# One tile of 64 columns for the two sliver tiles of a stick-breaking attention

## The chip, the cores and the metric

The kernel runs on one core of a Trainium2 chip. The metric is the device time of one execution in microseconds (us), the median of several runs. Engines are named as the profile names them: PE is TensorE's matmul, PEld its weight load, DVE is VectorE, ACT ScalarE, POOL GpSimd, and SP issues DMAs.

## The reference, cut to what matters

The program is one inference step of a hybrid decoder layer: stick-breaking attention in 8 heads beside gated linear attention (GLA) in 4 heads, with one input projection and one output projection. The change touches the prompt's stick-breaking attention alone. There are 16 meta tokens and 1024 prompt tokens; a query sees the keys strictly before it.

```
def stick_break_weights(z, mask):
    sp = jnp.where(mask, jax.nn.softplus(z), 0.0)
    later = lax.cumsum(sp, axis=z.ndim - 1, reverse=True) - sp
    return jnp.where(mask, jnp.exp(jax.nn.log_sigmoid(z) - later), 0.0)

def sb_attend(qb, qpos, k, v, kpos, bias):
    a = stick_break_weights(sb_logits(qb, k, bias), kpos[None, :] < qpos[:, None])
    return jnp.einsum('bhqk,bkhd->bqhd', a.astype(v.dtype), v)
```

The sum `later` runs over all keys after the current one that the query sees, so key tiles are worked from the last to the first, and each tile needs one number per query from the tile before: the sum so far.

## The kernel before, in words

Sizes: 1040 positions, head width 128, eight heads `h`. The queries of a head are split in two halves `qi`: positions 16 to 527 (qi = 0) and 528 to 1039 (qi = 1), 512 columns each. The keys are cut in tiles of `KT` = 126; tile `j` lies in columns 128 j to 128 j + 127 of `kt`, with zeros in its first and last row. The first row of a tile carries the sum of the tiles before it: its mask bias is -1e30, and the lower triangular matrix `ntri0` with a full first row adds it to every key.

For a key tile that reaches past the start of a query half, only the columns of the queries that can see it are worked. Half qi = 1 has the tiles j = 8 to 0 with 32, 158, 284, 410 and then five times 512 columns; half qi = 0 has j = 4 to 0 with 24, 150, 276, 402 and 512. The tiles (1, 8), 32 columns, and (0, 4), 24 columns, are the slivers. `ORDER` (L641) lists the tiles of a head: all of qi = 1, then all of qi = 0.

One tile is one generator, `attend_tile` (L578 to L629):

- three matmuls for the logits into a PSUM tile `z` (L589 to L591; every fp32 operand is held as a high and a low part, so a product takes three matmuls),
- softplus: DVE adds the bias and caps (L595), ACT does Exp and Ln (L596, L597), DVE adds and takes the maximum (L598), POOL masks with an affine select (L601),
- the carry of the tile before, read from row 0 of its `z` by ACT (L607), and the split in two parts by ACT and DVE (`split_tmp`, L574 and L575),
- two matmuls with `ntri0` onto `z` (L610, L611): the prefix sum,
- ACT's Exp to `Y` (L615), POOL's mask (L617), and the split again,
- three matmuls with the values onto the half's output `O` (L623 to L625); after j = 0 ACT copies `O` (L628) and SP stores it to `od`.

The `z` tiles come from a tag of four PSUM banks, `O` from one bank, and three more banks hold the projections' accumulators. The transposes of K and V to tokens (`tok_out`, L541, copied by L543 to L546) and the sample products (`sample_q`, L651 and L656) use the `z` tag too. A tile's bank becomes free when its last reader is done.

Order: a `Weaver` counts beats. The main program issues the projections (`inproj`, L342 to L344; six matmuls, then one beat) and each generator says after how many beats it goes on. Attention of head h is so woven between the V, K and Q projections of head h + 1. Within a tile the steps stand 2, then `D1` = 4, then `D2` = 6 beats apart, and a tile whose predecessor's carry is not yet there steps one beat at a time. Instructions of an engine run in the order in which they were issued to it. Beside this, DVE works through the sample scores (`z_feed`, L464), tied to the projections' progress by explicit dependencies.

`load_v` (L554 to L569) fetches a head's values from the output tensor through staging buffers (`stage`, seven of them) into `V`. `head` zeroes `kt` (L681, L682), and `split_k` (L685 to L697) fills it.

Of the kernel before, what the change touches and what calls it, by code (L numbers as in the profile page):

```python
# [10 lines left out]
F32 = mybir.dt.float32  # L11
# [5 lines left out]
ALU = mybir.AluOpType  # L17
# [3 lines left out]
P = 128  # L21
# [6 lines left out]
NSMP = NB * NT  # L28
T = META + SEQ + NSMP
REAL = META + SEQ  # L30
# [10 lines left out]
KT = 126  # L41
# [43 lines left out]
def hybrid_step(ctx: ExitStack, tc: tile.TileContext, x_prompt, x_sample, cache_k, cache_v, state_gla,  # L85
# [3 lines left out]
    nc = tc.nc  # L89
    mm = nc.tensor.matmul  # L90
    vec, act, pool = nc.vector, nc.scalar, nc.gpsimd
# [17 lines left out]
    W = Weaver()  # L109

    def stage(nm, dt=F32):
        return stg.tile([P, 384], dt, tag="stg", name=nm)
# [39 lines left out]
    znd = dram.tile([NSMP, HEADS, NSMP], F32, name="znd")  # L152
# [37 lines left out]
    with tc.tile_pool(name="xp", bufs=2) as xp, tc.tile_pool(name="xps", bufs=5, space=PSUM) as xps:  # L190
# [109 lines left out]
        for c, (lo, hi) in enumerate(XCHUNKS):  # L300
            n = hi - lo
            for k in range(NK):
                ps = xps.tile([P, 512], F32, tag="tx", name=f"tx{c}_{k}")
                ks = slice(k % 8 * P, (k % 8 + 1) * P)
                for j, i in enumerate(TILES[c]):
                    xt = xts[i]
                    if len(xt) == 2:
                        src, ii = xt[k // 8][:, ks], ident[:]
                    else:
                        rs = slice(64 * (k // 8), 64 * (k // 8) + 48)  # L310
                        src, ii = xt[0][rs, ks], ident[rs, rs]
# [215 lines left out]
    with tc.tile_pool(name="sp", bufs=1) as sp, tc.tile_pool(name="sps", bufs=1, space=PSUM) as sps:  # L527
# [26 lines left out]
        def load_v(h, V, behind):  # L554

            for c in range(3):
                st = stage(f"vr{h}_{c}")
                sv = st[:].rearrange("p (a d) -> p a d", d=P)
                nt = 3 if c < 2 else 2
                src = new_v_prompt[0, 0, :, h, :]  # L560
                pool.memset(st[:], 0.0)
                nc.sync.dma_start(sv[1:KT + 1, :nt], src[c * 378:c * 378 + nt * KT].rearrange("(a p) d -> p a d", p=KT))
                if c == 2:
                    nc.sync.dma_start(sv[1:33, 2, :], src[8 * KT:REAL])
                vs = slice(3 * c, 3 * c + 3)
                ins = act.copy(V[0][:, vs, :], sv)
                tc.add_manual_dep(ins.ins, behind.name, NOSYNC, reason="behind")
                vec.tensor_tensor(V[1][:, vs, :], sv, V[0][:, vs, :].bitcast(F32), ALU.subtract)
                yield 1  # L569

        def split_tmp(X, rows, n, nm):
            a = sp.tile([P, 512], F32R, tag="hi", bufs=3, name=f"hi_{nm}")
            b = sp.tile([P, 512], F32R, tag="lo", bufs=3, name=f"lo_{nm}")
            act.copy(a[:rows, :n], X)  # L574
            vec.tensor_tensor(b[:rows, :n], X, a[:rows, :n].bitcast(F32), ALU.subtract)  # L575
            return a, b

        def attend_tile(h, qi, qlo, qhi, j, jmax, q, kt, V, carry, O):  # L578
            nm = f"{h}_{qi}_{j}"
            k0 = j * KT  # L580
            nk = P
            c0 = max(qlo, k0)
            col = c0 - qlo
            n = qhi - c0
            qs = slice(c0 - META, c0 - META + n)
            ks = slice(j * P, j * P + nk)
            z = sps.tile([P, 512], F32, tag="z", bufs=4, name=f"z{nm}")
            zz = z[:nk, :n]
            mm(zz, kt[0][:, ks], q[0][:, qs], start=True, stop=False)  # L589
            mm(zz, kt[0][:, ks], q[1][:, qs], start=False, stop=False)  # L590
            mm(zz, kt[1][:, ks], q[0][:, qs], start=False, stop=True)  # L591
            bias = bias0[:nk, h:h + 1]
            xt = sp.tile([P, 512], F32, tag="X", bufs=3, name=f"X{nm}")
            X = xt[:nk, :n]
            vec.tensor_scalar(X, zz, bias, 30.0, ALU.add, ALU.min)  # L595
            act.activation(X, X, AF.Exp)  # L596
            act.activation(X, X, AF.Ln, bias=1.0)  # L597
            vec.scalar_tensor_tensor(X, zz, bias, X, ALU.add, ALU.max)  # L598
            w = min(n, k0 + KT - c0)
            if w > 0:  # L600
                pool.affine_select(X[:, :w], X[:, :w], [[1, w]], ALU.is_gt, 0.0, base=c0 - k0 + 1, channel_multiplier=-1)  # L601
            yield 2
            if j < jmax:
                while carry.get(qi, (None,))[0] != j + 1:
                    yield 1
                _, cz, ccol = carry[qi]
                act.activation(X[0:1, ccol - col:], cz[0:1, :], AF.Copy, scale=-1.0)  # L607
            sh, sl = split_tmp(X, nk, n, "s" + nm)
            yield D1
            mm(zz, ntri0[:nk, :nk], sh[:nk, :n], start=False, stop=False, skip_group_check=True)  # L610
            mm(zz, ntri0[:nk, :nk], sl[:nk, :n], start=False, stop=True, skip_group_check=True)  # L611
            carry[qi] = (j, zz, col)
            yt = sp.tile([P, 512], F32, tag="X", bufs=3, name=f"Y{nm}")
            Y = yt[:nk, :n]
            act.activation(Y, zz, AF.Exp, bias=bias)  # L615
            if w > 0:
                pool.affine_select(Y[:, :w], Y[:, :w], [[1, w]], ALU.is_gt, 0.0, base=c0 - k0 + 1, channel_multiplier=-1)  # L617
            ah, al = split_tmp(Y, nk, n, "a" + nm)
            yield D2
            if j == jmax:  # L620
                O[qi] = sps.tile([P, 512], F32, tag="O", name=f"O{h}_{qi}")
            o = O[qi]
            mm(o[:, col:], V[0][:nk, j, :], ah[:nk, :n], start=(j == jmax), stop=False, skip_group_check=True)  # L623
            mm(o[:, col:], V[0][:nk, j, :], al[:nk, :n], start=False, stop=False, skip_group_check=True)
            mm(o[:, col:], V[1][:nk, j, :], ah[:nk, :n], start=False, stop=(j == 0), skip_group_check=True)  # L625
            if j == 0:
                st = sp.tile([P, 512], F32, tag="X", bufs=3, name=f"ost{h}_{qi}")
                act.copy(st[:], o[:])  # L628
                nc.sync.dma_start(od[h][:, qlo - META:qhi - META], st[:])  # L629

        def attend(h, q, kt, V):

            carry, O = {}, {}
            for qi, j in ORDER:
                qlo, qhi = ((16, 528), (528, REAL))[qi]
                n = qhi - max(qlo, j * KT)
                W.spawn(attend_tile(h, qi, qlo, qhi, j, (qhi - 1) // KT, q, kt, V, carry, O))
                yield 2 if n < 100 else 3 if n < 200 else 4 if n < 450 else 5

        D1, D2 = 4, 6  # L640
        ORDER = [(1, j) for j in range(8, -1, -1)] + [(0, j) for j in range(4, -1, -1)]  # L641

        def values(h, behind):
            V = [sp.tile([P, 9, P], F32R, tag=f"V{i}", name=f"V{i}_{h}") for i in range(2)]
            W.spawn(load_v(h, V, behind))
            return V

        def sample_q(h, qsm, ks):

            ps = sps.tile([P, 512], F32, tag="z", bufs=4, name=f"qst{h}")  # L650
            nc.tensor.transpose(ps[:NSMP, 0:P], qsm[:], ident[:])  # L651
            qtok = stage(f"qtok{h}")[:NSMP, :P]
            act.copy(qtok, ps[:NSMP, 0:P])
            nc.sync.dma_start(qsd[:, h * P:(h + 1) * P], qtok)
            ps = sps.tile([P, 512], F32, tag="z", bufs=4, name=f"zn{h}")
            mm(ps[:NSMP, :NSMP], ks[:], qsm[:], start=True, stop=True)  # L656
            zns = sp.tile([NSMP, NSMP], F32, tag="zns", name=f"zns{h}")
            act.copy(zns[:], ps[:NSMP, :NSMP])
            nc.sync.dma_start(znd[:, h, :], zns[:])
            yield 4  # L660
            heads_ready.append(h)

        def head(h):
# [15 lines left out]
            kt = [sp.tile([P, KW], F32R, tag=f"k{i}", name=f"k{i}_{h}") for i in range(2)]  # L679
# [3 lines left out]
            ks = sp.tile([P, NSMP], F32, tag="ks", name=f"ks{h}")  # L683

            def split_k(raw, c, lo, hi):  # L685
                at, end = lo, min(hi, REAL)
                while at < end:
                    j, off = divmod(at, KT)
                    n = max(1, (end - at) // KT) if off == 0 else 1
                    w = min(KT - off, end - at)  # L690
                    d = [t[:, j * P:(j + n) * P].rearrange("p (a x) -> p a x", a=n)[:, :, off + 1:off + 1 + w] for t in kt]
                    r = raw[:, at - lo:at - lo + n * w].rearrange("p (a x) -> p a x", a=n)
                    act.copy(d[0], r)
                    vec.tensor_tensor(d[1], r, d[0].bitcast(F32), ALU.subtract)
                    at += n * w
                if c == 2:
                    act.copy(ks[:], raw[:, REAL - lo:hi - lo])  # L697
                return
                yield
# [21 lines left out]
            V = values(h, copied[-1])  # L721
# [15 lines left out]
    with tc.tile_pool(name="gp", bufs=1) as gp, tc.tile_pool(name="gps", bufs=1, space=PSUM) as gps:  # L737
# [323 lines left out]
        for g in range(GH):  # L1061
            kt = gp.tile([P, T], F32, tag="k", name=f"gk{g}")
# [629 lines left out]
```

## Time and profile before

| | us |
|---|---|
| median of 3 runs (2065.34 to 2067.61) | 2066.58 |
| the profiled execution, its own time | 2066.38 |
| its span, first to last instruction | 2064.6 |
| first to last logits product of the attention (L589) | 116.3 to 833.0 |
| mean granted clock of TensorE | 0.999 |

The busy times are summed from instruction records. Matmul records overlap, each next one starting before the one ahead has ended, so the distance from start to start is what a matmul costs TensorE, not its duration. In rows of the timeline the first number is the start in us from the span's start, the second the duration in us; a bracket at the end names how long the engine had been idle and for what.

### The profile page before, as it was taken

How to read it: one execution, taken by the hardware profiler on the slowest of the kernel's cores; microseconds unless marked ns; L12 is line 12 of the kernel's file. 1: busy time of each engine (PE TensorE's matmuls, PEld its weight loads, DVE VectorE, ACT ScalarE, POOL GpSimd, SP SyncE). 2: the span in 40 equal slices, each digit the busy share in tenths (PEclk: the TensorE clock that was granted, in tenths of full speed). 3: DMA queues.
4: the chain of work that ended last, by engine and by line, in shares of the span. 5: the costliest groups of instructions: out<-in, count | busy, mean ns of one | idle time of the engine just before them, and what ended most of it. 6: DMA issues, size and time to landing. Idle time of an engine off the chain costs nothing.

```text
span 2064.6 us, 41985 instructions
## 1 busy us (share of the span) xinstructions
PE 2024.8 (98%) x12507; PEld 1863.6 (90%) x12507; DVE 1552.7 (75%) x6282; ACT 953.4 (46%) x2293; POOL 84.6 (4%) x304
## 2 busy tenths in 40 slices
PE   6999999999999999999999999999999999999998
PEld 5999999999999998999999999998888898788776
DVE  7368989888988989899798897978544347454576
ACT  7355555565655656433534335343433325332332
POOL 0012000101000000000000000000000000000000
PEclk9999999999999999999999999999999999999999
DMA  6354454544455442533433433335776666452485
GB/s 202 103 139 148 139 159 133 171 132 147 146 160 146 140 124 76 139 102 82 108 100 79 125 82 110 98 82 155 236 233 231 220 222 200 139 166 74 129 271 202
DMA packets 371821, 301.85 MB, mean 146 GB/s; under 512 B 42360, under 2 KB 312104, under 8 KB 371592
## 3 DMA queue, kind: packets, MB, share of 16 engines
q1 hardware_dynamic: 371288, 298.64, 48.6%
q8 instruction: 98, 1.61, 0.3%
q14 instruction: 131, 1.07, 0.2%
q10 hardware_dynamic: 304, 0.53, 0.1%
HBM read 241.75 MB, written 57.31 MB: 145 GB/s over the span
## 4 chain that ended last, share of the span: by engine, by line
PE 75%; DVE 12%; DMA 6%; ACT 3%; issue 3%; SPq 0%; POOL 0%; DVEq 0%; ACTq 0%; POOLq 0%
PE acc_g L342 5%; PE acc_g L343 5%; PE acc_g L344 5%; DVE jk L464 5%; PE b L1593 4%; PE b L1595 4%; PE b L1594 4%; PE acc_k L342 3%; PE acc_k L344 3%; PE acc_k L343 3%; PE acc_v L342 2%; PE acc_q L342 2%; PE acc_q L344 2%; PE acc_q L343 2%; PE acc_v L344 2%
## 5 line engine op out<-in xcount | busy, mean ns | idle before, releaser
L464 DVE SCALAR_TENSOR_TENSOR jk<-kp,qb 128x128 f32<-128x128 f32 x2048 | 593.8, 290 | 43.5 <-DMA qb<-qsd 1.7
L342 PE MATMUL acc_g<-hT,wh_g 128*128 128x368 f32 (+2 forms) x768 | 251.4, 327 | 0.5 <-DVE ga L389 0.5
L343 PE MATMUL acc_g<-hT,wh_g 128*128 128x368 f32 (+2 forms) x768 | 247.6, 322 | 0.0
L344 PE MATMUL acc_g<-hT,wl_g 128*128 128x368 f32 (+2 forms) x768 | 247.1, 322 | 0.0
L1593 PE MATMUL b<-ring,f 128*128 128x512 f32 x416 | 164.3, 395 | 3.5 <-ACT gx L521 1.4
L464 DVE DVE_READ_ACCUMULATOR jk<-kp,qb 128x1 f32 x2048 | 167.6, 82 | 0.0
L1594 PE MATMUL b<-ring,f 128*128 128x512 f32 x416 | 162.6, 391 | 0.0
L1595 PE MATMUL b<-ring,f 128*128 128x512 f32 x416 | 162.1, 390 | 0.0
L342 PEld LDWEIGHTS acc_g<-hT,wh_g 128*128 128x128 f32 x768 | 144.5, 188 | 13.3 <-issue 10.8
L343 PEld LDWEIGHTS acc_g<-hT,wh_g 128*128 128x128 f32 x768 | 144.6, 188 | 1.1 <-issue 0.4
L1395 DVE TENSOR_TENSOR ring<-wr,ring 128x512 fp32r<-128x512 f32 x104 | 71.3, 689 | 98.4 <-ACT ring L1394 97.7
L344 PEld LDWEIGHTS acc_g<-hT,wl_g 128*128 128x128 f32 x768 | 144.5, 188 | 0.0
L342 PE MATMUL acc_gv<-hT,wh_gv 128*128 128x400 f32 (+2 forms) x384 | 130.5, 340 | 0.0
L1394 ACT CAST ring<-wr 128x512 fp32r<-128x512 f32 x104 | 64.1, 620 | 139.3 <-PE b L1595 77.0
L342 PE MATMUL acc_k<-hT,wh_k 128*128 128x384 f32 (+1 forms) x384 | 126.4, 329 | 0.0
L343 PE MATMUL acc_gv<-hT,wh_gv 128*128 128x400 f32 (+2 forms) x384 | 125.3, 326 | 0.0
L342 PE MATMUL acc_q<-hT,wh_q 128*128 128x368 f32 (+2 forms) x384 | 125.1, 326 | 0.0
L344 PE MATMUL acc_gv<-hT,wl_gv 128*128 128x400 f32 (+2 forms) x384 | 124.8, 325 | 0.0
L344 PE MATMUL acc_k<-hT,wl_k 128*128 128x384 f32 (+1 forms) x384 | 124.7, 325 | 0.0
L343 PE MATMUL acc_k<-hT,wh_k 128*128 128x384 f32 (+1 forms) x384 | 124.5, 324 | 0.0
L344 PE MATMUL acc_q<-hT,wl_q 128*128 128x368 f32 (+2 forms) x384 | 123.4, 321 | 0.0
L343 PE MATMUL acc_q<-hT,wh_q 128*128 128x368 f32 (+2 forms) x384 | 123.4, 321 | 0.0
(454 smaller groups left out, 5294.3 us busy)
## 6 DMA issues: line engine op xcount, KB each, us to landing
kp<-in_cache_k_dram SPq DMA_DIRECT2D x512, 64.0 KB
vr<-in_cache_v_dram SPq DMA_DIRECT2D x64, 512.0 KB
tf<-in_w_out_dram SPq DMA_DIRECT2D x64, 256.0 KB
td<-tf SPq DMA_DIRECT2D x64, 256.0 KB
qb<-qsd SPq DMA_DIRECT2D x64, 256.0 KB
wr_g<-in_w_in_dram SPq DMA_DIRECT2D x64, 256.0 KB
wr<-td SPq DMA_DIRECT2D x56, 256.0 KB
wr<-in_w_out_dram SPq DMA_DIRECT2D x48, 256.0 KB
```

The source lines that it names most:

```text
L342: mm(acc[c][:, :n], wh, hh[k][:, lo:hi], start=(k == 0), stop=False)
L343: mm(acc[c][:, :n], wh, hl[k][:, lo:hi], start=False, stop=False)
L344: W.mark = mm(acc[c][:, :n], wl, hh[k][:, lo:hi], start=False, stop=(k == NK - 1)).ins
L464: ins = vec.scalar_tensor_tensor(jk[:], kp[:], 1.0, qbs[h, b][:, t, :], ALU.mult, ALU.mult, accum_out=zt[:, t, NPG - 1 - i:NPG - i])
L1394: act.copy(wh, r)
L1395: vec.tensor_tensor(wl, r, wh.bitcast(F32), ALU.subtract)
L1593: mm(bk[:], ah, wh, start=first and k == 0, stop=False, skip_group_check=True)
L1594: mm(bk[:], ah, wl, start=False, stop=False, skip_group_check=True)
L1595: mm(bk[:], al, wh, start=False, stop=last and k == 7, skip_group_check=True)
```

## The change

The two slivers become one tile, j = 8, of 64 columns: the last 32 queries of each half.

- Its keys are the last keys, in rows 1 to 31 as before (the last of all, which no query sees, drops out), and after them, in rows 32 to 55, the 24 keys 504 to 527 of tile 4. The keys are copied by POOL within `kt`, the values come by one more DMA a head (24 rows).
- Its mask is one affine select over both halves and a memset of the first half's first 32 rows, once for `X` and once for `Y`.
- Its carry serves both halves: columns 0 to 31 for (0, 3), columns 32 to 63 for (1, 7).
- Its product with the values goes to columns 256 to 319 of its own `z` bank, ACT copies that to a small tile `ob`, and for each half DVE adds 32 columns of it to the copy of `O` before the store.
- `ORDER` loses (0, 4). Tile (1, 7) is now the first that writes `O` of its half, (0, 3) that of the other.
- The small tile `zns` of the sample logits becomes a staging buffer.

```
@@ load_v
                 if c == 2:
-                    nc.sync.dma_start(sv[1:33, 2, :], src[8 * KT:REAL])
+                    nc.sync.dma_start(sv[1:32, 2, :], src[8 * KT:REAL - 1])
+                    nc.sync.dma_start(sv[32:56, 2, :], src[4 * KT:4 * KT + 24])
@@ attend_tile
+            both = j == 8
             c0 = max(qlo, k0)
             col = c0 - qlo
-            n = qhi - c0
+            n = 64 if both else qhi - c0
+            def queries(t):
+                if both:
+                    return t[:].rearrange("p (a x) -> p a x", a=2)[:, :, 480:512]
+                return t[:, qs]
+
+            def causal(t):
+                if both:
+                    t = t.rearrange("p (a x) -> p a x", a=2)
+                    pool.affine_select(t, t, [[1 - 24, 2], [1, 32]], ALU.is_gt, 0.0, base=24, channel_multiplier=-1)
+                    pool.memset(t[0:32, 0, :], 0.0)
+                elif w > 0:
+                    pool.affine_select(t[:, :w], t[:, :w], [[1, w]], ALU.is_gt, 0.0, base=c0 - k0 + 1,
+                                       channel_multiplier=-1)
...
-            if j < jmax:
+            jmax = (3, 7)[qi]
+            if not both:
                 while carry.get(qi, (None,))[0] != j + 1:
                     yield 1
...
-            carry[qi] = (j, zz, col)
+            if both:
+                carry[0], carry[1] = (4, z[:, 0:32], 480), (8, z[:, 32:64], 480)
+            else:
+                carry[qi] = (j, zz, col)
...
+            if both:
+                o = z[:, 256:320]
+                mm(o, V[0][:, j, :], ah[:, :n], start=True, stop=False, skip_group_check=True)
+                mm(o, V[0][:, j, :], al[:, :n], start=False, stop=False, skip_group_check=True)
+                mm(o, V[1][:, j, :], ah[:, :n], start=False, stop=True, skip_group_check=True)
+                O[2] = sp.tile([P, 64], F32, tag="ob", name=f"ob{h}")
+                act.copy(O[2][:], o)
+                return
...
             if j == 0:
                 st = sp.tile([P, 512], F32, tag="X", bufs=3, name=f"ost{h}_{qi}")
                 act.copy(st[:], o[:])
+                vec.tensor_tensor(st[:, 480:512], st[:, 480:512], O[2][:, 32 * qi:32 * qi + 32], ALU.add)
                 nc.sync.dma_start(od[h][:, qlo - META:qhi - META], st[:])
@@ attend
-        ORDER = [(1, j) for j in range(8, -1, -1)] + [(0, j) for j in range(4, -1, -1)]
+        ORDER = [(1, j) for j in range(8, -1, -1)] + [(0, j) for j in range(3, -1, -1)]
@@ sample_q
-            zns = sp.tile([NSMP, NSMP], F32, tag="zns", name=f"zns{h}")
-            act.copy(zns[:], ps[:NSMP, :NSMP])
-            nc.sync.dma_start(znd[:, h, :], zns[:])
+            zns = stage(f"zns{h}")[:NSMP, :NSMP]
+            act.copy(zns, ps[:NSMP, :NSMP])
+            nc.sync.dma_start(znd[:, h, :], zns)
@@ split_k
                 if c == 2:
+                    for t in kt:
+                        pool.tensor_copy(t[:, 8 * P + 32:8 * P + 56], t[:, 4 * P + 1:4 * P + 25].bitcast(F32))
                     act.copy(ks[:], raw[:, REAL - lo:hi - lo])
```

More of the change, by code (lines that the diff above doesn't have):

```diff
@@ L576, in split_tmp, with attend_tile @@
             return a, b
-        def attend_tile(h, qi, qlo, qhi, j, jmax, q, kt, V, carry, O):
+        def attend_tile(h, qi, qlo, qhi, j, q, kt, V, carry, O):
             nm = f"{h}_{qi}_{j}"
@@ L581, in attend_tile @@
             nk = P
+            both = j == 8
             c0 = max(qlo, k0)
             col = c0 - qlo
-            n = qhi - c0
+            n = 64 if both else qhi - c0
             qs = slice(c0 - META, c0 - META + n)
             ks = slice(j * P, j * P + nk)
+            def queries(t):
[10 more added lines that the diff above has]
+                                       channel_multiplier=-1)
             z = sps.tile([P, 512], F32, tag="z", bufs=4, name=f"z{nm}")
             zz = z[:nk, :n]
-            mm(zz, kt[0][:, ks], q[0][:, qs], start=True, stop=False)
-            mm(zz, kt[0][:, ks], q[1][:, qs], start=False, stop=False)
-            mm(zz, kt[1][:, ks], q[0][:, qs], start=False, stop=True)
+            mm(zz, kt[0][:, ks], queries(q[0]), start=True, stop=False)
+            mm(zz, kt[0][:, ks], queries(q[1]), start=False, stop=False)
+            mm(zz, kt[1][:, ks], queries(q[0]), start=False, stop=True)
             bias = bias0[:nk, h:h + 1]
@@ L599, in attend_tile @@
             w = min(n, k0 + KT - c0)
-            if w > 0:
-                pool.affine_select(X[:, :w], X[:, :w], [[1, w]], ALU.is_gt, 0.0, base=c0 - k0 + 1, channel_multiplier=-1)
+            causal(X)
             yield 2
-            if j < jmax:
+            jmax = (3, 7)[qi]
+            if not both:
                 while carry.get(qi, (None,))[0] != j + 1:
@@ L615, in attend_tile @@
             act.activation(Y, zz, AF.Exp, bias=bias)
-            if w > 0:
-                pool.affine_select(Y[:, :w], Y[:, :w], [[1, w]], ALU.is_gt, 0.0, base=c0 - k0 + 1, channel_multiplier=-1)
+            causal(Y)
             ah, al = split_tmp(Y, nk, n, "a" + nm)
@@ L636, in attend @@
                 n = qhi - max(qlo, j * KT)
-                W.spawn(attend_tile(h, qi, qlo, qhi, j, (qhi - 1) // KT, q, kt, V, carry, O))
+                W.spawn(attend_tile(h, qi, qlo, qhi, j, q, kt, V, carry, O))
                 yield 2 if n < 100 else 3 if n < 200 else 4 if n < 450 else 5
         D1, D2 = 4, 6
-        ORDER = [(1, j) for j in range(8, -1, -1)] + [(0, j) for j in range(4, -1, -1)]
+        ORDER = [(1, j) for j in range(8, -1, -1)] + [(0, j) for j in range(3, -1, -1)]
         def values(h, behind):
```

## The prediction

> **What bounds the kernel now.** I read the page's busy shares and chain first, then the busy time by stretch, then what TensorE waited for in the stretch that holds the attention, then single rows of that stretch in order of time.
>
> ```profile
> span 2064.6 us, 41985 instructions
> ...
> PE 2024.8 (98%) x12507; PEld 1863.6 (90%) x12507; DVE 1552.7 (75%) x6282; ACT 953.4 (46%) x2293; POOL 84.6 (4%) x304
> ...
> PE 75%; DVE 12%; DMA 6%; ACT 3%; issue 3%; SPq 0%; POOL 0%; DVEq 0%; ACTq 0%; POOLq 0%
> ```
>
> TensorE is busy in 98% of the span and has 75% of the chain that ended last. A share over the whole span proves little about one stage, so the next view cuts it: the columns are busy time and count of PE, its weight loads, DVE, ACT and POOL, then the granted clock, the DMA share and GB/s.
>
> ```profile
> 112.00:860.00 748.00, 743.03 (x4548) 711.83 (x4547) 664.79 (x3022) 430.35 (x1037) 72.06 (x249) 1.00 0.48 139
> 860.00:1400.00 540.00, 537.60 (x3653) 517.91 (x3652) 469.01 (x2316) 219.06 (x601) 0.84 (x9) 1.00 0.38 99
> 1400.00:1800.00 400.00, 395.56 (x2509) 347.28 (x2511) 207.69 (x534) 157.69 (x333) 3.60 (x15) 1.00 0.64 205
> ```
>
> The prompt attention of the eight heads runs from 116 to 852 us, woven between the projections' matmuls. There PE lacks 748.0 - 743.0 = 5.0 us of being always busy, at clock 1.00. What it waited for in that stretch:
>
> ```profile
> PE z L611 <- DVE lo_s L575: 2.5, 9, 0.8
> PE z L610 <- ACT hi_s L574: 1.7, 4, 0.9
> PE acc_g L342 <- DVE ga L389: 0.5, 1, 0.5
> ```
>
> So time taken off TensorE's queue here moves everything behind it forward, and the two stretches that follow (99.6% and 98.9% busy) hand it on to the end: the projections there are paced by the same queue. DVE, at 664.8 of 748, is the next bound, 83 us away.
>
> **What goes: one sliver tile a head.** Each of the eight heads loses tile (0, 4) with its 24 columns: three logits products, two of the prefix sum, three with the values. The rows are start, duration, engine and line; since durations overlap, the price is read from starts. Head 1's tile:
>
> ```profile
> 260.81 0.17 PE L589 MATMUL z<-q,k 128*128 128x24 f32 x1
> 260.83 0.26 PE L590 MATMUL z<-q,k 128*128 128x24 f32 x1
> 260.95 0.26 PE L591 MATMUL z<-q,k 128*128 128x24 f32 x1
> 261.06 0.42 PE L342 MATMUL acc_k<-hT,wh_k 128*128 128x384 f32 x1
> 261.32 0.34 PE L343 MATMUL acc_k<-hT,wh_k 128*128 128x384 f32 x1
> 261.49 0.33 PE L344 MATMUL acc_k<-hT,wl_k 128*128 128x384 f32 x1
> ...
> 268.82 0.17 PE L610 MATMUL z<-hi_s,ntri 128*128 128x24 f32 x1
> ...
> 268.96 0.43 PE L342 MATMUL acc_k<-hT,wh_k 128*128 128x384 f32 x1
> 269.22 0.33 PE L343 MATMUL acc_k<-hT,wh_k 128*128 128x384 f32 x1
> ...
> 276.49 0.26 PE L623 MATMUL O<-hi_a,V 128*128 128x24 f32 x1
> ...
> 276.82 0.42 PE L342 MATMUL acc_q<-hT,wh_q 128*128 128x384 f32 x1
> 277.08 0.34 PE L343 MATMUL acc_q<-hT,wh_q 128*128 128x384 f32 x1
> ```
>
> A projection product of 384 columns takes 0.17 us from start to start (261.32 to 261.49). From the first logits product to the projection's second product pass 261.32 - 260.81 = 0.51 us, of which 0.17 are the projection's own: the three cost 0.34 us. The pair of the prefix sum costs 269.22 - 268.82 - 0.17 = 0.23 us. The three with the values cost 276.82 - 276.49 = 0.33 us (the late product after them would also be late behind the transposes that stand just ahead of them). Together 0.90 us a head, 8 x 0.90 = 7.2 us. If that late product is charged too (277.08 - 276.82 - 0.17 = 0.09 us) it is 0.99, or 7.9 us in all.
>
> **What stays, now 64 columns wide.** The merged tile stands where the 32-column one stood. Nearest wider row, 158 columns with the values:
>
> ```profile
> 229.96 0.23 PE L623 MATMUL O<-hi_a,V 128*128 128x158 f32 x1
> ...
> 230.26 0.38 PE L342 MATMUL acc_v<-hT,wh_v 128*128 128x384 f32 x1
> 230.47 0.34 PE L343 MATMUL acc_v<-hT,wh_v 128*128 128x384 f32 x1
> ```
>
> 230.47 - 229.96 - 0.17 = 0.34 us: 158 columns cost what 24 do, so 64 cost nothing more. The bounds are 0 and 0.01 us for this group, under 0.3 us in all if every group grew so. I take 0.
>
> **The z bank that is held longer.** The carry of the merged tile for the first half of the queries is read only when tile (0, 3) reaches its carry, nine tiles later. Until then its z bank is not free, and z has four. So a bank that the second half's tiles, the transposes of V and the sample products shared is gone for some 50 us of each head. I laid the allocation times of head 1 and the times of the last reads beside each other with one bank less. At most points 0.7 us or more remain; at these it does not:
>
> ```profile
> 131.73 0.40 PE L589 MATMUL z<-q,k 128*128 128x512 f32 x1
> ...
> 131.97 0.29 ACT L607 ACTIVATE X<-z 1x158 f32<-1x158 f32 x1
> ...
> 503.36 0.40 PE L589 MATMUL z<-q,k 128*128 128x512 f32 x1
> ...
> 504.20 0.29 ACT L607 ACTIVATE X<-z 1x158 f32<-1x158 f32 x1
> ...
> 244.86 0.57 ACT L607 ACTIVATE X<-z 1x512 f32<-1x512 f32 x1
> ...
> 245.11 0.49 PE L541 MATMUL tk_v<-ident,vraw 128*128 128x128 f32 x3
> ...
> 246.28 0.49 PE L541 MATMUL tk_v<-ident,vraw 128*128 128x128 f32 x3
> ...
> 246.88 0.46 ACT L543 COPY st_v<-tk_v 128x384 f32<-128x384 f32 x1
> ...
> 247.32 0.39 PE L589 MATMUL z<-q,k 128*128 128x512 f32 x1
> ```
>
> Tile (1, 4) would take the bank of tile (1, 7), whose last read is the carry of 158 columns: in head 0 that ends at 132.26 and the tile starts at 131.73, 0.53 us too early; in head 4 it ends at 504.49 against 503.36, 1.13 us. And tile (1, 1), at 247.32, would need the bank that the copy of the second transposes leaves at 246.88 + 0.46 = 247.34: about even, and I charge 0.08 us for each of seven heads, an estimate. Sum 0.53 + 1.13 + 0.56 = 2.2 us of TensorE waiting. It is 0 if the order of instructions moves so that projections fill the gap. If the second transposes (245.11) get the bank whose carry read ends at 244.86 + 0.57 = 245.43, 0.32 us too late, seven heads pay 2.2 us more: 4.4 us. I take 2.2, since the repeating pattern of the heads gives the program order little reason to move.
>
> **The rest, costed at nothing, with its cover.**
>
> ```profile
> L575 DVE TENSOR_TENSOR lo_s<-X,hi_s x112: 173/578/695, 118.5 to 843.0; 128x512 fp32r<-128x512 f32 x48, 128x32 fp32r<-128x32 f32 x8, 128x158 fp32r<-128x158 f32 x8, 128x284 fp32r<-128x284 f32 x8
> ...
> L598 DVE SCALAR_TENSOR_TENSOR X<-z,bias,X x112: 238/639/752, 117.6 to 837.6; 128x512 f32<-128x512 f32 x48, 128x32 f32<-128x32 f32 x8, 128x158 f32<-128x158 f32 x8, 128x284 f32<-128x284 f32 x8
> ...
> 213.97 0.21 POOL L601 TENSOR_SCALAR_AFFINE_SELECT X<-X 128x32 f32<-128x32 f32 x1 [11.72 <-DVE X L598]
> ...
> 218.09 0.18 PE L610 MATMUL z<-hi_s,ntri 128*128 128x32 f32 x1
> ...
> 279.01 0.20 POOL L682 MEMSET k<- 128x128 f32 x1
> ...
> 298.27 0.38 SPq L629 DMA_DIRECT2D od<-ost  x1
> ```
>
> DVE loses four small operations a head (the minima above: about 0.24 + 0.24 + 0.17 + 0.17 = 0.82 us, 6.6 us in all) and gets two additions of 32 columns a head, between 0.17 and 0.24 us each, 2.7 to 3.8 us: still 3 us less. They stand between ACT's copy of O and the store to od; behind a waiting one, DVE's next operations queue, and its 83 us of idle time cover them. Without that cover it would be 16 x 0.24 = 3.8 us.
> ACT loses five operations a head and gets one copy; it idles 318 us here.
> POOL loses two selects and gets two memsets and two copies of key columns a head, each around the 0.20 us above. The memsets lengthen the merged tile's chain by some 0.2 us in front of ACT's split, twice; in head 1 the mask ended at 213.97 + 0.21 = 214.18 and the prefix sum began at 218.09, so it is hidden. The key copies queue ahead of masks of tiles (0, 1) and (0, 0); uncovered, 16 x 0.20 = 3.2 us.
> SP gets one more issue a head, at 0.38 us like the row, 3 us on a queue that mostly waits for others. The values it brings are needed only at the merged tile's last products, after both its masks and its prefix sum.
> The sample logits now leave through one of the seven staging buffers; if none were free, DVE would start a head's sample scores later. I see no such wait and take 0.
> The carry chain of the first half is one link shorter. What is late next is tile (0, 1): the waits on lo_s quoted above come mostly at its 402-column products. They may go or come back elsewhere: -3 to +3 us, taken as 0.
>
> **The sum.** -7.2 + 0 + 2.2 = -5.0 us. The profiled execution took 2066.38 us by its own time (2064.6 of span and 1.8 around it), 0.2 under the runs' median of 2066.58. From it, 2066.4 - 5.0 = 2061.4.
>
> **The rivals.**
> 1. The held bank costs nothing, because other work fills the gaps: -7.2 us, 2059.2. For it speaks that PE found work to do in nearly every gap so far; against it, that the three places above lie within about a microsecond.
> 2. The held bank starves TensorE. If the three transposes, needing a bank in close order, reuse the one just left, the third (246.28) waits for the copy that ends at 247.34, 1.06 us, and tile (1, 1) for the copy after, another 0.45 us: 1.5 us for each of seven heads, 10.6 us, on top of the 1.7 us of heads 0 and 4. -7.2 + 12.3 = +5.1, 2071.5. It decides from 0.9 us a head on, where the gain is used up. Against it: in the rows above the third transposes start before the second's copy has begun, so these two already sit on different banks.
> 3. The change saves less than it seems. The first two sliver products start 0.02 us apart; if each product cost only that, the eight heads would save 64 x 0.02 = 1.3 us, 2065.1. Against it: the second and third start 0.12 us apart, with 24 columns. [...]
> 4. The lo_s waits shrink as the chain shortens: -7.2 - 3 + 0, 2056.2.
>
> **How the numbers follow.** The forecast (2061.4, own range 2058 to 2064) gets 0.48, rival 1 gets 0.18, rival 2 0.12, rival 3 (or any other give-back that leaves about nothing) 0.14, rival 4 0.08. Two runs of this kernel can be told apart from about 0.2%, 4.1 us: faster means under 2062.4, slower over 2070.7. Of the forecast some two thirds lie under 2062.4, 0.33; with rivals 1 and 4 faster has 0.59. Slower is rival 2, 0.12. The rest, 0.29, is the same. The range runs from rival 4, 2056, to 2069, short of rival 2's centre.
>
> **What would show it.** Right: PE has 64 fewer products and weight loads, (0, 3) follows directly on (1, 0), and the stretch of the attention is 5 to 7 us shorter with the later stretches as long as before. The held bank: new waits of PE at L589 or L541 for ACT's carry copies and st_v, 2 us in sum; over 7 us of them would be rival 2. POOL's key copies ahead of a mask that lo_s waits for, or DVE waiting at the new addition with PE behind it, would show a cover that failed. A later stretch that grows by what the attention saves would mean that TensorE's queue was not what paced it.

## The result, and the profile after

| | before | changed |
|---|---|---|
| median of 12 runs each, us | 2066.53 | 2072.59 |
| ratio, 95% interval | | 1.0030 (1.0022 to 1.0038) |
| span of the profiled execution, us | 2064.6 | 2069.3 |

The changed kernel is slower by 0.3%, 6 us, where 5 us less was forecast: beyond the range, whose upper end was 2069. One of its twelve runs took 5120 us, for a reason that no trace shows, and doesn't enter the ratio. Each ratio below stands against runs of the kernel before on the same chip, so ratios are compared, not medians.

The head of the page and the three stretches of the changed kernel:

```profile
span 2069.3 us, 41783 instructions
...
PE 2025.1 (98%) x12443; PEld 1859.0 (90%) x12443; DVE 1550.6 (75%) x6266; ACT 946.9 (46%) x2261; POOL 89.1 (4%) x320
```

```profile
112.00:860.00 748.00, 736.73 (x4458) 700.96 (x4457) 658.21 (x2980) 422.92 (x1003) 73.69 (x248) 1.00 0.49 138
860.00:1400.00 540.00, 537.79 (x3650) 518.21 (x3649) 469.97 (x2328) 217.22 (x595) 2.90 (x24) 1.00 0.38 99
1400.00:1800.00 400.00, 396.01 (x2509) 348.55 (x2507) 207.04 (x542) 156.70 (x335) 3.60 (x15) 1.00 0.64 206
```

12507 - 12443 = 64 products are gone, as the change says. In the attention's stretch PE is idle for 748.0 - 736.7 = 11.3 us where it was 5.0; the two stretches behind are as busy as before. So the loss is made in the attention. What the weight loads waited for there, from 112 to 870 us, first before, then changed (total, times, longest):

```profile
PEld z L611 <- DVE lo_s L575: 6.2, 13, 1.1
PEld z L610 <- ACT hi_s L574: 3.3, 5, 1.2
PEld zn L656 <- issue: 2.2, 8, 0.3
PEld acc_g L342 <- DVE ga L389: 0.7, 1, 0.7
PEld acc_v L342 <- ACT qsm L718: 0.2, 1, 0.2
```

```profile
PEld z L627 <- DVE lo_s L576: 8.2, 18, 0.9
PEld z L626 <- ACT hi_s L575: 5.0, 7, 2.6
PEld z L605 <- ACT X L623: 3.8, 4, 1.3
PEld z L605 <- ACT st_v L543: 2.6, 7, 0.4
PEld zn L683 <- issue: 2.2, 8, 0.3
PEld acc_v L342 <- ACT qsm L747: 1.9, 3, 1.1
PEld acc_g L342 <- DVE ga L389: 0.7, 1, 0.7
```

(In the changed file L605 is the first logits product, L623 the carry read, L626 and L627 the prefix sum, L575 and L576 the split, L601 the mask, L747 the sample queries' copy.) The two rows L605 are the held bank and are new. But hi_s, lo_s and qsm have grown too.

Each head has one pair of sample products `zn`, just ahead of its attention; from one to the next is one head. The first and the eighth, before and changed:

```profile
118.77 0.25 PE L656 MATMUL zn<-qsm,ks 128*32 128x32 f32 x2
...
769.03 0.25 PE L656 MATMUL zn<-qsm,ks 128*32 128x32 f32 x2
```

```profile
118.86 0.25 PE L683 MATMUL zn<-qsm,ks 128*32 128x32 f32 x2
...
773.83 0.25 PE L683 MATMUL zn<-qsm,ks 128*32 128x32 f32 x2
```

Seven head spans took 650.3 us and take 655.0: +4.7, which is the whole growth of the span (2069.3 - 2064.6). From each span I take the weight loads' waits in it (all but the issue waits at `zn`); the remainder is the time in which TensorE had its next operand:

| seven heads, us | waits | remainder | sum |
|---|---|---|---|
| before | 8.8 | 641.5 | 650.3 |
| changed | 20.3 | 634.7 | 655.0 |
| difference | +11.5 | -6.8 | +4.7 |

**In the profiled execution the products saved what was forecast, 6.8 / 7 = 0.97 us a head against 0.90, and the waits took it all and 4.7 us more.** Of the 11.5 us, 6.4 are the held bank, 3.4 hi_s and lo_s, 1.8 qsm. The rest of this document asks why.

### The profile page after: what moved, and what is told of

Its sections match the earlier page's. It is cut to its first block, busy times and chain, and to the rows that moved or that the text cites. A ratio compares the mean times of both kernels' runs of the same rounds, so it can differ in the third digit from the quotient of the medians.

```text
span 2069.3 us, 41783 instructions
## 1 busy us (share of the span) xinstructions
PE 2025.1 (98%) x12443; PEld 1859.0 (90%) x12443; DVE 1550.6 (75%) x6266; ACT 946.9 (46%) x2261; POOL 89.1 (4%) x320
## 3 DMA queue, kind: packets, MB, share of 16 engines
q14 instruction: 130, 1.06, 0.2%
## 4 chain that ended last, share of the span: by engine, by line
PE 71%; DVE 13%; DMA 5%; issue 4%; ACT 4%; POOL 1%; SPq 1%; DVEq 0%; POOLq 0%; ACTq 0%
PE acc_g L342 5%; PE acc_g L343 5%; PE acc_g L344 5%; DVE jk L464 5%; PE b L1622 4%; PE b L1624 4%; PE b L1623 4%; PE acc_k L342 3%; PE acc_k L343 3%; PE acc_k L344 3%; PE acc_q L343 2%; PE acc_q L342 2%; PE acc_q L344 2%; PE acc_gq L342 2%; PE acc_gq L343 2%
```

## The experiments

The same two columns for every kernel, with its ratio to the kernel before. "Kept beats" means that tile (0, 3) is spawned two beats later and waits two more, so that the first half runs at the beats that it had before the change:

| kernel | ratio (95% interval) | waits | remainder |
|---|---|---|---|
| e4 drop: before without tile (0, 4) | 1.0002 (0.9993 to 1.0011) | 14.4 | 636.7 |
| e6 drop, kept beats | 0.9978 (0.9968 to 0.9987) | 9.9 | 635.2 |
| e5 before, meant to hold the bank (it didn't) | 1.0005 (0.9996 to 1.0014) | 8.3 | 641.8 |
| e9 before, bank held | 1.0012 (1.0003 to 1.0021) | 12.1 | 640.5 |
| changed | 1.0030 (1.0022 to 1.0038) | 20.3 | 634.7 |
| e1 changed, first half's carry saved | 1.0026 (1.0015 to 1.0036) | 18.2 | 639.6 |
| e2 changed, keys by ACT and DVE | 1.0035 (1.0022 to 1.0048) | 21.8 | 636.2 |
| e7 changed, kept beats | 1.0017 (1.0008 to 1.0026) | 19.9 | 636.8 |
| e8 e7, output in another tile's bank | 1.0034 (1.0022 to 1.0046) | 18.1 | 636.4 |
| e10 e7, bank given back early | 1.0007 (0.9998 to 1.0016) | 17.3 | 634.8 |
| e11 e10 without the small additions | 1.0007 (0.9998 to 1.0016) | 15.2 | 636.5 |
| f1 e6 with a 64-column first tile | 1.0003 (0.9994 to 1.0012) | 12.3 | 635.0 |
| e12 e10, key copies on DVE | 1.0000 (0.9991 to 1.0009) | 15.9 | 636.4 |
| e13 e12, V's memsets on DVE | 0.9988 (0.9979 to 0.9997) | 15.3 | 635.1 |
| f4 e13 without kept beats | 1.0018 (1.0009 to 1.0027) | 16.5 | 635.6 |
| f5 before, V's memsets on DVE | 0.9994 (0.9985 to 1.0003) | 7.3 | 641.4 |

Every kernel with one tile less has a remainder of 634.7 to 636.8, but for e1 (below, under the hardware); every kernel with the tile 640.5 to 641.8. The waits run from 7.3 to 21.8. In these seven heads the work is the forecast's wherever the tile is gone, and the waits make the difference. But waits and remainder come from one execution of each kernel, and leave out what follows the eighth `zn`: that took from 1294.5 us (e2) to 1300.3 (e6, whose granted clock was 0.71 and 0.72 at 1438 to 1450 us). So what a version is worth is read from the ratios, and the table only shows where in the heads it comes from.

**The tile alone (e4) and with its beats kept (e6).** e4's edit:

```
-ORDER = [(1, j) for j in range(8, -1, -1)] + [(0, j) for j in range(4, -1, -1)]
+ORDER = [(1, j) for j in range(8, -1, -1)] + [(0, j) for j in range(3, -1, -1)]
-W.spawn(attend_tile(h, qi, qlo, qhi, j, (qhi - 1) // KT, q, kt, V, carry, O))
+W.spawn(attend_tile(h, qi, qlo, qhi, j, (3, 8)[qi], q, kt, V, carry, O))
```

> The kernel before without tile (0, 4) and with nothing in its place (24 keys are left out for 24 queries; nothing else changes). The term of 0.90 us a head says 7.2 us less than before, about 2059.3 us, and 64 products fewer. If a sliver product costs only the 0.02 us of its first row, 2065 us. If the time comes out as before, what TensorE saves here is given back somewhere and the removed tile was never worth anything.

Median 2067.6, ratio 1.0002: no gain, although nothing was put in the tile's place. But its heads' spans had become shorter by 0.4 to 1.0 us in five of seven cases, and longer by 2.5 and 2.3 us in two, those of head 0 and head 4. e6 adds

```
 for qi, j in ORDER:
+    if (qi, j) == (0, 3): yield 2          # attend, ahead of the spawn
...
-yield 2
+yield 4 if (qi, j) == (0, 3) else 2        # attend_tile, behind the mask of X
```

> The kernel before without tile (0,4), whose part of the result is left out, but with the beats of the other tiles as they were: (0,3) is spawned two beats later than in the plain drop, and its prefix sum comes two beats later still (48 instead of 44). In the plain drop five of the seven spans from one head's zn to the next had become 0.4 to 1.0 us shorter, as forecast, but the two from head 0 and from head 4 had grown by 2.5 and 2.3 us. Theory 'weave': the four beats by which the chain of the first half became shorter put its masks and splits into other places of POOL's and ACT's queues, and that gives the time back; with the beats kept the 0.9 us a head stays: 2059.3 us (2066.5 - 7.2). Rival 'no gain': the tile lay in the shadow of something else, and the time stays at 2066 to 2067.5 with the beats kept too.

Ratio 0.9978, 4.5 us faster: the saving is real once the beats stay, and the intervals of e4 and e6 don't touch. Where the two part is seen on POOL in head 0, first e4, then e6:

```profile
189.14 0.66 POOL L601 TENSOR_SCALAR_AFFINE_SELECT X<-X 128x110 f32<-128x110 f32 x1 [3.86 <-DVE X L598]
189.77 0.88 POOL L401 TENSOR_SCALAR_AFFINE_SELECT lv<-lv 128x64 f32<-128x64 f32 x2
190.60 0.41 POOL L561 MEMSET vr<- 128x384 f32 x1
190.97 0.83 POOL L403 TENSOR_SCALAR_AFFINE_SELECT lv<-lv 128x64 f32<-128x64 f32 x2
191.76 0.29 POOL L617 TENSOR_SCALAR_AFFINE_SELECT Y<-Y 128x126 f32<-128x126 f32 x1
```

```profile
187.13 1.45 POOL L401 TENSOR_SCALAR_AFFINE_SELECT lv<-lv 128x64 f32<-128x64 f32 x2
188.54 0.41 POOL L561 MEMSET vr<- 128x384 f32 x1
188.91 0.83 POOL L403 TENSOR_SCALAR_AFFINE_SELECT lv<-lv 128x64 f32<-128x64 f32 x2
189.69 0.42 POOL L561 MEMSET vr<- 128x384 f32 x1
190.06 0.29 POOL L617 TENSOR_SCALAR_AFFINE_SELECT Y<-Y 128x126 f32<-128x126 f32 x1
```

With the chain four beats shorter, the mask of tile (0, 0)'s X has moved ahead in POOL's queue and waits 3.86 us for DVE; the selects that build the level masks (`lv`) and V's memsets stand behind it, and the mask of tile (0, 1)'s Y, which the next split needs, behind those. ACT splits that Y ahead of the X of (0, 0), so the prefix sum of (0, 0) pays 2.49 us at its weight load. In e6 the selects run without that wait ahead of them. The mask behind them is that of (0, 2)'s Y, the prefix sum of (0, 1) pays 1.33 us (1.23 in the kernel before), and that of (0, 0) waits for nothing. The two weight loads, e4 and e6:

```profile
193.17 0.19 PEld L610 LDWEIGHTS z<-hi_s,ntri 128*128 128x128 f32 x1 [2.49 <-ACT hi_s L574]
```

```profile
191.28 0.19 PEld L610 LDWEIGHTS z<-hi_s,ntri 128*128 128x128 f32 x1 [1.33 <-ACT hi_s L574]
```

The changed kernel has the same queue at 191 us (mask of X at 191.03, behind 2.39 us of waiting for DVE, the mask of Y at 193.65) and the same wait, 2.57 us. This is head 0 alone: the level masks are built only once in the program. In e4's head 4 the waits grow by some 3 us as well, in several rows (the largest are 1.06 us at a prefix sum of the second half and 0.96 us for qsm); their origin wasn't traced.

**The held bank by itself (e5, e9).** e5 was to hold the last tile's bank in the kernel before by one more read of it in tile (0, 3), and missed:

```
+if j == 8: carry[2] = z[:, 0:32]
...
+if (qi, j) == (0, 3): act.copy(held_[:], carry[2][0:1, :])
```

> The kernel before, whole, with one more small ACT copy in tile (0, 3) that reads row 0 of the z bank of tile (1, 8), so that this bank stays taken until there, as in the changed kernel; nothing else of the change. Held-bank theory: the weight-load waits for a bank that the changed kernel shows (6.4 us: about 1 us at tile (1, 4) in three heads, 0.37 us at tile (1, 1) in seven) come here too, about 2073 us. Rival, that POOL's key copies and the later values cost the time: no more than the added copies, 2067 us. My prediction's own ledger: 2.2 us, 2068.7.

Ratio 1.0005 (0.9996 to 1.0014), and no wait at the logits. The trace shows why: the copy, written in tile (0, 3), ran at 123.91, right behind the carry read of tile (1, 7), because nothing made it wait. The bank wasn't held.

```profile
123.83 0.17 ACT L607 ACTIVATE X<-z 1x32 f32<-1x32 f32 x1
123.91 0.16 ACT L609 COPY held__835<-z 1x32 f32<-1x32 f32 x1
```

e9 makes the read need X of (0, 3): `act.activation(held_[:], carry[2][0:1, :], AF.Exp, bias=X[0:1, 0:1])`.

> The kernel before, with one more small ACT instruction a head, in tile (0,3): it reads the last tile's z bank, and needs X of (0,3), so it can't run before X is there and the bank is held as long as in the changed kernel. Nothing is left out. By the forecast's price of a held bank 2066.5 + 2.2 = 2068.7; by the changed kernel's rows (6.4 of weight-load waits) 2073; if the bank costs nothing 2066.5 to 2067.

```profile
PEld z L613 <- DVE lo_s L575: 5.4, 12, 1.1
PEld z L589 <- ACT st_v L543: 2.7, 7, 0.4
PEld z L589 <- ACT X L607: 2.4, 2, 1.2
...
PEld z L612 <- ACT hi_s L574: 2.1, 3, 1.2
```

Both of the changed kernel's new rows are here, 5.1 us in sum: at tile (1, 1) in seven heads, as there, and at tile (1, 4) in heads 0 and 4, where the changed kernel has heads 1 and 5 too. The ratio is 1.0012, 2.5 us (0.6 to 4.3 by its interval): part of it is bought back, since lo_s and hi_s wait 2.0 us less than before. The forecast had 2.2 for the price in time.

**The bank given back (e1, e8, e10).** e1 saves the first half's carry row:

```
+cr = sp.tile([P, NSMP], F32, tag="qsm", name=f"cr{h}")
+act.copy(cr[0:1, :], z[0:1, 0:32])
-carry[0], carry[1] = (4, z[:, 0:32], 480), (8, z[:, 32:64], 480)
+carry[0], carry[1] = (4, cr, 480), (8, z[:, 32:64], 480)
```

> The changed kernel, but ACT saves the carry of the first half (32 numbers) to SBUF after the merged tile's prefix sum, and tile (0, 3) reads it there; so the z bank is free after the copy of the merged output. Held-bank theory: the 6.4 us of waits mostly go, the ones at (1, 4) perhaps not wholly, since the bank is still held some 5 us longer than before; 2066 to 2067.5 us. If POOL's copies are the cause: unchanged, 2072 us.

The st_v row (2.6 us) is gone, the row of X stays at 3.4, since the merged output still lies in the bank when tile (1, 4) needs one; the ratio, 1.0026, can't be told from the change's. e8 keeps the beats, saves the carry and puts the merged output into free columns of tile (1, 7)'s bank:

> The changed kernel with the beats kept, and the merged tile's z bank given back early: the first half's carry row is copied to SBUF, and the merged output goes to free columns of tile (1,7)'s z bank. Theory 'weave' with a held bank: both kinds of new wait are gone, and the saving of the removed tile is left: 2059 to 2061.5. If the bank cost only the forecast 2.2, this is 2 us under the kernel with the beats kept; if 6.4, 6 us under it. Rival 'no gain': 2070 or more.

```
+if (qi, j) == (1, 7): carry[2] = z
...
-o = z[:, 256:320]
+o = carry[2][:, 256:320]
```

It missed: the output's first product now waits until the carry has been read from that bank, a new row in place of the old ones.

```profile
PEld z L646 <- ACT X L625: 7.6, 8, 2.2
PEld z L628 <- ACT hi_s L575: 7.4, 5, 1.9
PEld z L629 <- DVE lo_s L576: 4.1, 9, 0.5
```

e10 has e1's saved carry and kept beats, leaves the output where the change has it, and runs its three products two beats earlier:

```
-yield D2
+yield 4 if both else D2
```

> The changed kernel with the beats of the first half kept, the first half's carry row copied to SBUF, and the merged tile's three value products two beats earlier (at beat 10 of its head, not 12), so that its z bank is free before tile (1,4) needs one. Theory 'the bank is one of several causes': the 4.8 us of waits for X and st_v of the kernel with kept beats (2071.0) go, and nothing takes their place: 2066 to 2067.5; the waits for hi_s and lo_s stay at 14 us. Rival 'the bank is all': 2063.4, the time of the drop with kept beats. Rival 'a freed wait is given back elsewhere', as in the run with the early release: 2071.

Both bank rows are gone. The ratio is 1.0007, against 1.0017 for e7 (the change with kept beats and nothing else):

> The changed kernel, with the beats of the first half kept as they were before the change (the same two edits at (0,3)). Theory 'weave': the waits for hi_s, lo_s and qsm go back to those of before, the held bank stays: 6.4 us of weight-load waits for the carry reads and st_v, so 2059.3 + 6.4 - 0.4 = about 2065 us (2061.4 if the bank costs only the forecast 2.2). Rival 'no gain': the time stays near 2072.

```profile
PEld z L626 <- ACT hi_s L575: 8.5, 9, 1.8
PEld z L627 <- DVE lo_s L576: 7.4, 17, 0.7
PEld z L605 <- ACT st_v L543: 2.6, 7, 0.4
PEld z L605 <- ACT X L623: 2.2, 2, 1.2
...
PEld acc_v L342 <- ACT qsm L749: 0.3, 1, 0.3
```

```profile
PEld z L626 <- ACT hi_s L575: 10.3, 9, 1.8
PEld z L627 <- DVE lo_s L576: 6.7, 15, 0.8
...
PEld acc_v L342 <- ACT qsm L751: 1.7, 2, 1.4
```

From e7 (first) to e10, 4.8 us of bank waits go, hi_s and qsm grow by 3.2, lo_s falls by 0.7: freeing the bank is worth some 2 us (1.0017 to 1.0007, intervals overlapping). Kept beats are worth 2.7 us by e7 against the change (overlapping), and 6 us by f4 against e13 (below), whose intervals don't touch. f4 is e13 without the two edits at (0, 3):

> The kernel of e13_memset (bank given back early, key copies and V's memsets on DVE) without the kept beats: (0,3) runs at the beats that the change gives it. Theory 'weave', of the drop's two versions (2067.6 against 2063.4): 2 to 4 us above e13_memset, 2068 to 2070. Rival: with POOL's queue free of memsets and copies the beats make no difference, 2065 to 2067.

So the beats have their price even where POOL has neither the key copies nor V's memsets in its queue. Where f4 pays it isn't located: the seven head spans of the two profiles differ by 1.6 us (652.0 and 650.4).

**What is left: the small additions, the width, POOL's queue (e2, e11, f1, e12, e13, f5).** With beats and bank put right, e10 is still 6 us above e6. e2 took the key copies off POOL in the changed kernel as it is:

```
-pool.tensor_copy(t[:, 8 * P + 32:8 * P + 56], t[:, 4 * P + 1:4 * P + 25].bitcast(F32))
```

(both parts are made again from `kraw` instead, by a cast on ACT and a subtraction on DVE).

> The changed kernel, but the 24 keys go into tile 8 from the raw projection by one ACT cast and one DVE subtraction (as all other keys do), not by two POOL copies inside kt. If POOL's copies, which wait for DVE's split and have the staging memsets of V behind them, make V late and hold ACT in front of the q evacuation: the waits for qsm (1.9 us) and part of the added hi_s and lo_s waits (3.7 us) go, 2067 to 2070.5 us. Held-bank theory alone: unchanged, 2072 us, and the waits at L605 stay.

No gain, 1.0035. e11 takes e10 and leaves out the key copies, V's second transfer and the addition at the end:

```
-pool.tensor_copy(t[:, 8 * P + 32:8 * P + 56], t[:, 4 * P + 1:4 * P + 25].bitcast(F32))
-nc.sync.dma_start(sv[32:56, 2, :], src[4 * KT:4 * KT + 24])
-vec.tensor_tensor(st[:, 480:512], st[:, 480:512], O[2][:, 32 * qi:32 * qi + 32], ALU.add)
```

> The kernel of e10_early without the copies of 24 keys on POOL, the second transfer of V's last chunk and the addition on DVE at the end: what is left is the merge itself (the first half's part of the merged tile is computed without its keys and not added, so the output lacks it). If these three small additions feed the longer waits for hi_s and lo_s, 2063 to 2064, as the drop with kept beats; if the merged tile itself does (its mask in two instructions, its copies on ACT), the time of e10_early.

The same ratio as e10, though the qsm row is gone. So the additions aren't the six microseconds. f1 widens the first tile of e6 to 64 columns, without the two copies on ACT and without the merged output. Two things of the change come with the width: the mask's second instruction, POOL's memset, and the staging buffer for `zns`. Against the changed kernel, cut to two places:

```
-carry[0], carry[1] = (4, cr, 480), (8, z[:, 32:64], 480)
+carry[1] = (8, z[:, 32:64], 480)
...
-o = z[:, 256:320]
-mm(o, V[0][:, j, :], ah[:, :n], start=True, stop=False, skip_group_check=True)
+o = O[qi][:, 480:]
+mm(o, V[0][:, j, :], ah[:, 32:64], start=True, stop=False, skip_group_check=True)
```

> The kernel of e11_bare with the tile of the last keys still 64 columns wide (logits, X, mask in two instructions, prefix sum, Y), but without the copies on ACT that the merge needs (carry row to SBUF, output to SBUF), and with value products of the second half's 32 columns alone, straight into O[1]: the drop with kept beats, with a wider first tile. The first half's part is left out. If the width itself feeds the waits, 2069, as e11_bare; if the two copies on ACT do, 2063 to 2064.5, as the drop with kept beats (the value trio at 32 columns runs in both).

Ratio 1.0003: with the 64-column tile, e6's gain of 4.5 us is gone (the intervals don't touch). The profiles show 2.3 us of that (head spans 645.1 and 647.3 us), mostly in head 1, whose waits go from 1.3 to 3.1 us at the prefix sums of the second half. There the trace shows more than the width, on POOL and ACT, first e6, then f1:

```profile
212.99 0.21 POOL L601 TENSOR_SCALAR_AFFINE_SELECT X<-X 128x32 f32<-128x32 f32 x1 [11.66 <-DVE X L598]
...
213.24 0.22 ACT L574 CAST hi_s<-X 128x32 fp32r<-128x32 f32 x1 [0.56 <-POOL X L601]
```

```profile
213.26 0.24 POOL L597 TENSOR_SCALAR_AFFINE_SELECT X<-X 128x64 f32<-128x64 f32 x1 [12.79 <-DVE X L613]
213.45 1.71 POOL L403 TENSOR_SCALAR_AFFINE_SELECT lv<-lv 128x64 f32<-128x64 f32 x2
215.12 0.11 POOL L598 MEMSET X<- 32x32 f32 x1
...
215.26 0.24 ACT L574 CAST hi_s<-X 128x64 fp32r<-128x64 f32 x1 [2.17 <-POOL X L598]
```

The last level mask's selects, which e6 runs at 200 us, stand between the two instructions of the mask in f1: the memset of 0.11 us starts 1.6 us after the select has ended, and hi_s of the merged tile comes 2.0 us later than in e6, where head 1 as a whole is 0.4 us later. What stands behind it on ACT and DVE stays late, down to the hi_s of tile (1, 5) (229.96 and 232.58). The same row of 1.71 us stands in the same place in the changed kernel and in e10, e11 and e13. So by the trace most of what the profiles show of f1's loss goes back to the mask's second instruction. That is argued, not tested: no run has the width with a mask in one instruction. The rest isn't located.

e12 takes e10's key copies from POOL to DVE, and e13 V's memsets too:

```
-pool.tensor_copy(t[:, 8 * P + 32:8 * P + 56], t[:, 4 * P + 1:4 * P + 25].bitcast(F32))
+vec.tensor_copy(t[:, 8 * P + 32:8 * P + 56], t[:, 4 * P + 1:4 * P + 25].bitcast(F32))
...
-pool.memset(st[:], 0.0)
+vec.memset(st[:], 0.0)
```

> The kernel of e10_early with the copies of the 24 keys on DVE instead of POOL. Theory 'POOL's queue': in tiles (0,1) and (0,0) hi_s waits on ACT behind hi_a, which waits for POOL's mask, which stands behind the key copies (0.37 us) and V's memsets (0.42 us each); without the copies about 0.3 us a head less wait for hi_s: 1.5 to 2.5 us under e10_early. Rival: DVE, at 89% busy, gives it back as lo_s waits: the same time as e10_early.

> The kernel of e12_keysdve with V's three memsets a head (0.42 us each on POOL) on DVE too, so that POOL has nothing but masks in its queue there. Theory 'POOL's queue': the waits for hi_s in tiles (0,1) and (0,0), 5 us and more, fall under 3, and the time comes 2 to 4 us under e12_keysdve, about 2062. Rival: the waits for lo_s grow by as much, since DVE's queue takes the memsets, and the time stays.

```profile
PEld z L627 <- DVE lo_s L576: 10.5, 15, 1.4
PEld z L626 <- ACT hi_s L575: 3.6, 5, 1.2
```

e12's ratio is 1.0000 (e10: 1.0007, not told apart). In e13 hi_s waits fall from e10's 10.3 us to 3.6, and lo_s waits rise from 6.7 to 10.5: more than half of it moved from ACT's waits to DVE's. Its 0.9988 is the one version of the merge below the kernel before. The control f5, the kernel before with the memset line of e13 alone, asks whose gain that is:

> The kernel before with V's three memsets a head on DVE instead of POOL, and nothing else. It tells how much of e13_memset's 2065.9 is the merge and how much the memsets. If hi_s waits (3.3 us) go and lo_s waits don't grow: 2064 to 2065, so that the merge itself still brings nothing; if the memsets only trade one wait for another: 2066.5 to 2068, and e13_memset's gain is the merge's.

0.9994 (0.9985 to 1.0003): the interval holds both no gain and nearly all of e13's, and the two intervals overlap. A gain of the merge itself isn't shown by any kernel here.

## Why the prediction was wrong, by its steps

- **The removed tile, -7.2 us: right as work.** 0.97 us a head in the changed kernel, 0.90 in e6 ((641.5 - 635.2) / 7), against 0.90. Rival 3, that it saves almost nothing, falls as far as it speaks of the products' cost. What was wrong is to hand the term to the end: e4 takes the tile out, keeps the work's saving, and gains nothing; e6, with the beats kept, hands on 4.5 us of the 7.2 (2.7 to 6.6 by its interval).
- **64 columns, at 0, with two memsets of "some 0.2 us", "hidden": a step that failed.** For TensorE it is right, the remainders show no cost (635.0 us in f1, 635.2 in e6). But f1, which adds this to e6, is 5.1 us slower than e6 by the ratios (1.0003 against 0.9978). The memsets were taken as hidden, since the merged tile's own prefix sum came 3.9 us behind the mask. In f1's head 1 the mask ends 1.7 us after its select instead of 0.2. Its own prefix sum hides even that; but ACT and DVE stand still behind it, and the prefix sums of (1, 6) and (1, 5) wait 2.3 us where e6 has no wait. The rest of the 5.1 isn't located.
- **The held bank, +2.2: the right tiles, and the right time by e9 (2.5) with some luck.** Tile (1, 1) waits 0.37 us seven times, where 0.08 was charged, and tile (1, 4) waits in four heads, not two, 3.8 us where 1.7 was charged: 6.4 us of waits in the changed kernel. e9 shows why the time is less than the waits: other waits shrink behind them, which the term left out. Rival 2, a starved TensorE, has the right sign, and its 0.45 us at tile (1, 1) is near the 0.37 measured; but most of it lay at the transposes, which have no row among the waits. That its 2071.5 lies near the measured time is luck.
- **The chain, "-3 to +3 us, taken as 0": the other step that failed.** It was treated as noise around zero. The waits for hi_s and lo_s grew by 3.4 us and by 1.8 for qsm, which had no term; and e4 against e6 (1.0002 to 0.9978) prices the four beats by themselves at 5 us (in the changed kernel e7 buys back 2.7, not clear of the noise). Rival 4 had the opposite sign.
- **"The rest, at nothing":** key copies, transfer and addition together can't be told from nothing (e11 against e10). But for the masks that queue behind the key copies no cover was named, and POOL's queue matters: e13, which clears it of the copies and of V's memsets, takes two thirds of e10's hi_s waits away, of which DVE gives more than half back.
- **The reading under it.** The prediction took TensorE's waits from the matmul rows, 4.7 us in the attention; the weight loads' rows in the same trace had 12.6, 2.2 of them "issue" at `zn`. With 4.7 us of waits there seemed little that could grow. In this trace the matmuls' busy time hid the rest: PE looked 99.3% busy there (743.0 of 748), the weight loads 95.2% (711.8), and only their rows show the other 5.7 us of waits for operands.
- **The range.** Its upper end left out that several of these come at once; only rival 2 reached past it.

Open are the part of f1's loss that no wait shows, where the beats cost what they do outside head 0, and how much of the changed kernel's 6 us each cause holds. Taken one at a time, the removed tile (-4.5 by e6), the beats (+5.0), the 64-column tile (+5.1) and the bank (+2.5) come to +8.1: the steps needn't add up, since in e7, e9, e10 and e13 a wait that went let another grow, or the reverse.

## What to carry to other kernels

In a hand-woven order of in-order queues, work taken out of the bounding engine is only worth what the waits leave of it: try the removal by itself first, with the old timing of everything else kept (e6) and without (e4), and the difference is the price of the weave (here 0.9978 against 1.0002). Count the bounding engine's waits where its operands are awaited (here at the weight loads, 12.6 us before the change, where the matmul rows had 4.7), divide every stretch into work and waits, and ask of each queue that a step has moved in what now stands ahead of it and for what that waits. A small tile that two chains share holds its bank until the later one has read it (6.4 us of waits in the changed kernel), and an instruction added to its chain, however short (here a memset of 0.11 us), can land behind work that has nothing to do with it (1.71 us of selects in f1).

## What the runs showed of the hardware

Behind some of the longer waits the clock granted to TensorE was lower. In e4, behind 2.49 us, it was 0.76 from 192 to 198 us; in the changed kernel, behind 2.57 us at the same place, it stayed at 1.00 (the last three columns are granted clock, DMA share and GB/s):

```profile
192.00:198.00 6.00, 4.28 (x16) 3.92 (x17) 5.12 (x26) 2.83 (x5) 2.83 (x7) 0.76 0.41 113
```

```profile
192.00:198.00 6.00, 3.19 (x17) 2.53 (x16) 4.01 (x22) 1.98 (x4) 2.83 (x10) 1.00 0.41 123
```

In e4 the products of 304 columns then start 0.25 us apart, against 0.14 in the changed kernel, which kept its clock. The length of the wait alone doesn't decide it: in e7, where no wait of the attention is above 1.8 us, the clock was 0.74 in the same stretch. What sets it isn't shown by these runs.

Part of the remainders' scatter goes with such falls. Head 0 of e4, which has the one above, has a remainder of 92.3 us, its other heads 90.5 to 90.9. Of the other kernels with one tile less, e11 had a clock of 0.73 from 656 to 662 us, e8 of 0.91 and 0.80 from 656 to 668, e1 of 0.72 and 0.71 from 192 to 204, and e7, beside the stretch above, of 0.72 from 662 to 668. With e4 these have remainders of 636.4 to 639.6, e1's the largest. The changed kernel, at 1.00 in all of its seven heads, has 634.7.
